# Two queues for the transposed blocks: SBUF-to-SBUF transfers issued by SP or ScalarE

## The chip, the cores and the metric

The kernel runs on one core of a Trainium2 chip. The metric is the device time of one execution in microseconds, median of several runs. The core has a matrix engine (TensorE, PE in the profile, its weight loads PEld), VectorE (DVE), ScalarE (ACT), GpSimd (POOL) and SyncE (SP). Each has its own instruction queue, which runs in order. DMAs are issued by instructions in the queues of SP and ScalarE and carried out by 16 DMA engines that all queues share; SP does nothing else in this kernel, while ScalarE also computes.

## The reference

Two layers (DEPTH = 2) of a decoder trunk, 512 positions of width 1024, in float32:

```python
mod = c_silu @ w_ada + b_ada                  # shift, scale, gate
u = rms_norm(x, norm_g) * (1 + scale) + shift
z = u @ w_in                                  # one projection, split for all mixers
ya = dsa_attention(rope(aq), rope(ak), av, rope(iq), rope(ik), iw) * silu(ag)
yb = swa_sinks_attention(rope(bq), rope(bk), bv, sinks) * silu(bg)
yc = stick_breaking_attention(cq, ck, cv) * silu(cg)
merged = sigmoid(ma) * (ya @ w_br_a) + sigmoid(mb) * (yb @ w_br_b) + sigmoid(mc) * (yc @ w_br_c)
x = x + gate * (merged @ w_out)
```

Mixer a has 8 heads of 64; an indexer scores the keys and each query attends, with a softmax, to its 128 best ones. Mixer b is a softmax attention over a window of 128 keys with a learned sink, 8 query heads on 2 key heads. Mixer c is a stick-breaking attention with 8 heads. A last RMSNorm follows.

## The kernel before

Activations lie transposed: features on the 128 partitions, the 512 positions along the free side. For precision every factor of a matrix product is split into a high and a low part of type float32r, and three products are added (high by high, high by low, low by high). So a weight block of 128x512 is loaded by a DMA (tile `wstage`, 4 buffers), cast to its high part (`whi`, on ScalarE, VectorE or GpSimd), and the rest is subtracted (`wlo`). PE then multiplies it with `uh` and `ul`, the two parts of u, into the banks `ps_z`.

The program has, for each layer, a first phase, a phase for the values, the mixers c, b and a, and the output projection. In the mixers several streams run woven together: the projections of the heads, the branches' products (`w_br_*`), the gates, the modulation of the next layer (`w_ss`, in layer 0), the indexer and its top-k (VectorE's max and match_replace on `score`), and the attention itself, pair of heads by pair of heads.

Queries and keys of the mixers a and b are rotated in `rope_evac` (L909-917): the projection is copied from its bank to `zs`, four DMAs swap the halves of each head from `zs` to `m2` (the profile calls it `m`), and VectorE or GpSimd combines them to `zc`, from which `Q` and `KH` are split.

For each of the four pairs of heads of mixers b and a, `softmax_qk` (L1262) computes the scores and the exponentials, and writes the normalised weights into one tile X (128 partitions, 1792 columns for b, 2560 for a; one buffer). Before they meet the values these weights must be transposed. `softmax_tr32` (L1356-1371) does it in two steps: VectorE transposes all 32x32 blocks within a quarter of X (4 instructions of 128x448 or 128x640), and after each of these 4 DMAs move 32 partitions of that quarter to another place in a tile U, or in `V5` (the profile calls it `V`) for the odd pairs. So a pair has 16 DMAs from SBUF to SBUF, 4 behind each transpose, all written as SP's. There are 2 layers x 2 mixers x 4 pairs = 16 such rows, 256 DMAs. The products with the values read U or V (`pairs`, L618). Mixer c transposes on PE (`softmax_tr`, L1372) and its rows have no such DMA. `TR32` (L47) says which pairs go through `softmax_tr32`: all four of a and all four of b.

The order is not that of the text. A `Recorder` takes each instruction with its alternatives (`add`, L317: a dictionary from engine to operation) and prices each one (`price`, L358). `forward` (L431) then plans the whole program: at each step the engine that can start an instruction earliest takes it, and among those ready the one with the earliest due time. An instruction with alternatives goes to the engine where it would end first (`elsewhere`, L558). For a DMA the price is the time on the issuing engine (`cost`) and the time of its bytes (`lag`, at 385 GB/s); its end is planned at L522-529, with a latency and behind the DMA before it. `LANES = 8`: the plan lets SP wait for the eighth DMA before it. `latest` computes due times from the plan, and `order` repeats this 5 times and keeps the plan that ends first. `emit` (L609) writes the instructions in that order, so each engine's queue is fixed. L620 is the line that emits nearly all of them, which is why most rows of the profile name it.

ScalarE issues 8 DMAs before, the stores `xsave<-xm` to HBM in `save`; all others are SP's.

Of the kernel before, what the change touches and what calls it, by code (L numbers as in the profile page):

```python
# [25 lines left out]
F32 = mybir.dt.float32  # L26
# [6 lines left out]
S = 512  # L33
P = 128
# [247 lines left out]
class Recorder:  # L282
# [75 lines left out]
    def price(self, x, engine, op, args, kw):  # L358

        y = Way()  # L360
        y.op, y.args, y.kw, y.mode, y.port = op, args, kw, None, False
        o = x.writes[0] if x.writes else None
        if op == "preload_act_table_set":
            y.cost = y.lag = 1.3
            return y
        if op == "dma_start":
            n = 1
            for d in (o or x.reads[0]).shape:
                n *= d
            y.cost, y.lag, y.mode = (0.58 if x.reads and x.writes and not x.reads[0].tile.pool.fixed else 0.36) if engine == "SP" else 0.1, n * 4 / 385e3, "dma"  # L370
            return y
        n = 1
        for d in o.shape[1:]:
            n *= d
        from_psum = any(v.tile.pool.name[:3] == "ps_" for v in x.reads)
        if engine == "PE":
            if op == "pairs":
                w = [int(np.prod(q[2].shape[1:])) for q in args]
                low, full = ([v for v, q in zip(w, args) if (q[2].dtype == F32) == t][::2] for t in (False, True))
                c, y.mode = sum(4 * v / 2.4e3 for v in full) + sum((v + 33) / 2.4e3 for v in low), "c" if full else "r"  # L380
                c += 0.37 if full and low else 0.26 if low else 0.21
                y.cost, y.lag = c, c + self.PIPE
            elif op == "transpose":
                c, y.mode = 0.1085, "t"
                y.cost, y.lag = c, c + self.PIPE
            else:
                rhs, y.mode = args[2], "m"
                c = 4 * n / 2.4e3 + 0.01 if rhs.dtype == F32 else 0.06 if rhs.dtype == BF16 else max(0.112, (n + 33.5) / 2.4e3)
                y.cost, y.lag = c, c + self.PIPE
            return y  # L390
        accum = "accum_out" in kw
        if engine == "ACT":
            b = 0.09 * sum(isinstance(kw.get(k), View) for k in ("bias", "scale"))
            c = 0.205 + 0.83e-3 * n + (b if not accum else 0.18) - (0.04 if from_psum else 0)
        elif engine == "DVE":
            y.port = not from_psum and op not in ("max", "match_replace", "memset", "reciprocal")
            if op == "tensor_tensor_scan":
                c = 1.21
            elif op == "max":
                c = 0.15 + 1.05e-3 * args[1].shape[-1]  # L400
            elif op == "match_replace":
                c = 0.215 + 1.045e-3 * args[2].shape[-1]
            elif n <= 16:
                c = 0.27 if op == "tensor_scalar" and len(x.reads) > 2 else 0.22 if op == "tensor_scalar" else 0.165 + (0.1 if accum else 0)
            elif op == "tensor_tensor_reduce":
                c = 0.147 + 1.05e-3 * n
            elif from_psum:
                c = 0.147 + 1.05e-3 * n + (0.08 if accum else 0)
            elif op in ("tensor_scalar", "tensor_copy"):
                c = 0.225 + 0.45e-3 * n if op == "tensor_scalar" else 0.16 + 0.52e-3 * n  # L410
            elif op == "memset":
                c = 0.1 + 0.6e-3 * n
            else:
                c = 0.15 + 1.05e-3 * n + (0.0 if accum else 0.06 if op == "scalar_tensor_tensor" else 0.0)
        else:
            y.port = n > 16
            if op == "memset":
                c = 0.12 if n < 16 else 0.52
            elif op == "tensor_copy":
                c = 0.2 + 0.82e-3 * n  # L420
            elif op == "tensor_scalar":
                c = 0.2 + 2.8e-3 * n
            else:
                c = 0.1 + 2.35e-3 * n
        y.cost, y.lag = c - self.OVERLAP[engine], c
        if engine != "POOL" and o.shape[0] < P:
            y.cost = c + (0.08 if engine == "DVE" else 0.02)
        return y


    def forward(self):  # L431
        E = {e: {"free": 0.0, "port": 0.0, "mode": None, "ready": {}, "pend": []} for e in self.real}
        dma_free, lanes = 0.0, []
# [36 lines left out]
        while len(out) < len(self.list):  # L470
            best = None
            for name, e in E.items():
# [5 lines left out]
                for i in list(ready):  # L478
                    x = ready[i]
# [3 lines left out]
                    y = x.alts[name]  # L483
                    at = max(free, port) if y.port else free
# [5 lines left out]
                if mine is None or mine[0] > free + 1e-9:  # L490
                    while pend and self.list[pend[0][1]].taken:
                        heapq.heappop(pend)
                    if pend:
                        est, i = pend[0]
                        x = self.list[i]
                        at = max(est, port) if x.alts[name].port else est
# [11 lines left out]
            e, x = E[name], self.list[i]  # L508
            y = x.alts[name]
# [12 lines left out]
            if y.mode == "dma":  # L522
                if not x.writes:
                    x.end = at + 2.1
                else:
                    x.end = dma_free = max(at + (2.1 if at < 20.0 else 3.0), dma_free) + y.lag * (1.2 if dma_free < 5.5 else 1.0)
                lanes.append(x.end)
                if name == "SP" and len(lanes) >= self.LANES:
                    e["free"] = max(e["free"], lanes[-self.LANES])
            else:  # L530
                x.end = at + y.lag + (hold - y.cost)
# [99 lines left out]
def op(cost, fn, *chunks):  # L631
    return ("op", cost, fn, [c + (phase[0],) for c in chunks])
# [15 lines left out]
def trunk(ctx, tc, xT, vecs, w_ss, w_gt, w_first, w_t, w_v, w_br, w_o, rope, consts, out):  # L648
# [7 lines left out]
    rec = Recorder(tc, nc, ps, sb)  # L656
    PE, ACT, DVE, POOL, SP = (rec.engine(e) for e in ("PE", "ACT", "DVE", "POOL", "SP"))
# [7 lines left out]
    def sbank():  # L665
        return rec.tile("ps_s", [P, S])
# [4 lines left out]
    def t512(tag, bufs=None, dt=F32):  # L671
        return rec.tile(tag, [P, S], dt)
# [38 lines left out]
    csb, o = small[:, 0:8], 8  # L711
    g_sb = [small[:, o + 8 * l:o + 8 * l + 8] for l in range(L)]
    fg_sb, o = small[:, o + 8 * L:o + 8 * L + 8], o + 8 * L + 8
    b_ada, o = [small[:, o + 24 * l:o + 24 * l + 24] for l in range(L)], o + 24 * L
    sink, o = small[:, o:o + 8 * L], o + 8 * L
# [59 lines left out]
    st = {}  # L775
# [560 lines left out]
    def blocks(b):  # L1336
        return 14 if b == "b" else 20
# [18 lines left out]
    def softmax_tr32(b, p):  # L1356
        def fn():
            pt = st.pop(("p", p))
            pos = bpos if b == "b" else apos
            N = blocks(b)  # L1360
            X = pt
            U = st["V5"][:, :N * P] if p % 2 and b in ('a', 'b') else rec.tile("U", [P, N * P], F32)
            n = N * 32
            for b_ in range(4):
                q = X[:, n * b_:n * b_ + n]
                DVE.transpose(q, q)
                for a_ in range(4):
                    SP.dma_start(U[32 * b_:32 * b_ + 32, n * a_:n * a_ + n], X[32 * a_:32 * a_ + 32, n * b_:n * b_ + n])
            st["pt", p] = U
        return op(1520 if b == "b" else 2180, fn)  # L1370

    def softmax_tr(b, p):  # L1372
        if p in TR32.get(b, ()):
            return softmax_tr32(b, p)

        def fn():
            pt = st.pop(("p", p))
            pos, tpos = (bpos, btpos) if b == "b" else (apos, cpos)
            nb = 4 if b == "b" else 5
            tb, PT, left = [None] * nb, [None] * nb, [0] * nb  # L1380
            for e in range(2):
                for j in range(4):
                    left[tpos(e, j)[0]] += 1
            for e in range(2):
                for j in range(4):
                    bk, c0 = tpos(e, j)
                    if tb[bk] is None:
                        tb[bk] = sbank()
                    for i in (range(j, min(4, j + 2)) if b == "b" else range(j, 4)):
                        sbk, s0 = pos(e, i)  # L1390
                        kc = s0 + 128 * j - keys(b, i)[0]
                        PE.transpose(tb[bk][:, c0 + 128 * (i - j):c0 + 128 * (i - j) + 128], pt[sbk][:, kc:kc + 128], ident)
                    left[bk] -= 1
                    if not left[bk]:
                        W = 384 if b == "b" and bk >= 2 else 512
                        if b == "c" and all(v is None for v in PT):
                            whole = rec.tile("U", [P, 5 * S], F32)
                        PT[bk] = whole[:, S * bk:S * bk + S] if b == "c" else t512("t", 10)
                        cast(PT[bk][:, :W], tb[bk][:, :W])
            st["pt", p] = PT  # L1400
        return op(1520 if b == "b" else 2180, fn)
# [402 lines left out]
```

## Time and profile before

| | |
|---|---|
| time, median of 3 runs | 1161.24 us (1161.12 to 1162.6) |
| the profiled execution | 1160.48 us, span 1158.7 us |
| mean granted clock of PE | 0.992 |
| PE busy | 1128.7 us (97%) |
| VectorE, ScalarE, GpSimd busy | 980.8, 547.0, 154.1 us |
| DMA moved | 157.23 MB, mean 136 GB/s |
| the chain that ended last | PE 79%, VectorE 12%, DMA 4%, SP's queue 2%, issue 2% |

The span is the time from the first to the last instruction. Busy PE means that a matmul is in its pipeline, not that it works at its peak. An instruction that issues a DMA is not counted as busy time of its engine; it shows in the timeline of the queue (SPq, ACTq), with the time that the issue took. The chain follows the work that ended last back to what released it at each step.

The mixers b and a lie at about 220 to 500 us in layer 0 and 800 to 1060 us in layer 1.

### The profile page before, as it was taken

Reading aid. Unit: us, or ns where it says so; the run is one execution under the profiler, and the core shown is the slowest. Engines: PE = TensorE matmul, PEld = TensorE weight load, DVE = VectorE, ACT = ScalarE, POOL = GpSimd, SP = SyncE. Lnnn points to the kernel's source line nnn. Section 1 sums busy time; section 2 is a strip of 40 time slices with the busy share of each in tenths; the row PEclk is TensorE's granted clock in tenths of the full one; section 3 lists DMA queues with packets and bytes.
Section 4 is the critical chain, followed back from the end, with each engine's and each line's share of the span. In section 5 each row is a group of like instructions: output and inputs, shape, how many; then the busy total and the mean of one; then the engine's idle time right before and its main releaser. Section 6 shows DMA issues by size and latency. Waiting matters only on the chain.

```text
span 1158.7 us, 17527 instructions
## 1 busy us (share of the span) xinstructions
PE 1128.7 (97%) x5619; PEld 935.8 (81%) x5619; DVE 980.8 (85%) x2223; ACT 547.0 (47%) x1150; POOL 154.1 (13%) x227
## 2 busy tenths in 40 slices
PE   8999999999997999999999999999999999999997
PEld 6899878888885777878898998888888777787886
DVE  7977999999998887878686689999999989776765
ACT  5623677653445552432143137765535456533222
POOL 0100345201012110000000004551000211000001
PEclk9999999999998999999999999999999999999999
DMA  9744323344454456555633342234445444535343
GB/s 346 234 117 128 97 77 92 109 144 129 129 161 144 140 158 174 148 166 165 188 120 108 103 134 82 82 92 124 130 146 142 132 108 137 160 107 145 95 126 107
DMA packets 92764, 157.23 MB, mean 136 GB/s; under 512 B 14080, under 2 KB 28672, under 8 KB 92672
## 3 DMA queue, kind: packets, MB, share of 16 engines
q1 hardware_dynamic: 91520, 154.02, 45.0%
q10 hardware_dynamic: 1152, 2.10, 0.5%
q8 instruction: 44, 0.72, 0.3%
q14 instruction: 48, 0.39, 0.1%
HBM read 125.39 MB, written 4.19 MB: 112 GB/s over the span
## 4 chain that ended last, share of the span: by engine, by line
PE 79%; DVE 12%; DMA 4%; SPq 2%; issue 2%; ACT 1%; POOL 0%; DVEq 0%; ACTq 0%
PE ps_z L620 60%; PE ps_s L620 15%; PE ps_s L618 3%; SPq L620 2%; DVE wlo L620 2%; DVE X L620 2%; PE ps_z L618 1%; DVE t L620 1%; DMA wstage<-in_w_t 1%; DVE zc L620 1%; DVE m L620 1%; DVE score L620 1%; DVE Q L620 1%; DMA Y<-in_w_ss 1%; DMA m<-zs 1%
## 5 line engine op out<-in xcount | busy, mean ns | idle before, releaser
L620 PE MATMUL ps_z<-uh,whi 128*128 128x512 f32 (+1 forms) x905 | 356.0, 395 | 10.4 <-DVE G L620 4.9
L620 PE MATMUL ps_z<-ul,whi 128*128 128x512 f32 (+1 forms) x905 | 354.2, 392 | 0.3 <-DVE ul L620 0.3
L620 PE MATMUL ps_z<-uh,wlo 128*128 128x512 f32 (+1 forms) x905 | 353.6, 392 | 0.0
L620 DVE TENSOR_TENSOR wlo<-wstage,whi 128x512 fp32r<-128x512 f32 (+2 forms) x329 | 215.1, 656 | 16.1 <-ACT whi L620 9.3
L620 PEld LDWEIGHTS ps_z<-uh,whi 128*128 128x128 f32 x905 | 170.9, 189 | 46.4 <-DVE G L620 5.2
L620 PEld LDWEIGHTS ps_z<-uh,wlo 128*128 128x128 f32 x905 | 171.0, 189 | 35.0 <-issue 0.7
L620 PEld LDWEIGHTS ps_z<-ul,whi 128*128 128x128 f32 x905 | 171.2, 189 | 34.5 <-issue 0.7
L620 ACT CAST whi<-wstage 128x512 fp32r<-128x512 f32 (+2 forms) x144 | 86.8, 606 | 154.7 <-PE ps_z L620 73.3
L620 DVE CAST whi<-wstage 128x512 fp32r<-128x512 f32 (+2 forms) x179 | 71.9, 402 | 94.2 <-PE ps_z L620 68.9
L620 PE MATMUL ps_z<-Y,whi 128*128 128x512 f32 x384 | 119.8, 392 | 1.3 <-DVE Y L620 1.0
L620 ACT ACTIVATE e<-ps_z 128x512 f32<-128x512 f32 x68 | 40.4, 595 | 105.7 <-PE ps_z L620 103.8
L620 PEld LDWEIGHTS ps_z<-Y,whi 128*128 128x128 f32 x384 | 72.3, 189 | 17.4 <-DVE Y L620 1.4
L620 ACT ACTIVATE e<-e 128x512 f32<-128x512 f32 x96 | 59.6, 629 | 45.5 <-DVE e L620 43.3
L620 ACT ACTIVATE t<-t,nm 128x256 f32<-128x256 f32 (+3 forms) x128 | 65.2, 511 | 21.6 <-DVE nm L620 21.6
L620 PE MATMUL ps_z<-Y,wlo 128*128 128x512 f32 x192 | 74.9, 390 | 0.0
L620 POOL CAST whi<-wstage 128x512 fp32r<-128x512 f32 (+1 forms) x49 | 29.9, 610 | 328.6 <-PE ps_z L620 229.8
L620 ACT ACTIVATE t<-t 128x512 f32<-128x512 f32 x120 | 67.2, 629 | 1.4 <-POOL zc L620 0.5
L620 POOL TENSOR_TENSOR wlo<-wstage,whi 128x512 fp32r<-128x512 f32 (+2 forms) x43 | 54.8, 1274 | 94.8 <-PE ps_z L620 61.8
L620 PE MATMUL ps_s<-KH,Q 128*128 128x256 f32 (+3 forms) x280 | 51.7, 305 | 5.9 <-DVE e L620 3.5
L620 DVE MAX8 m<-score 128x8 f32<-128x384 f32 (+2 forms) x96 | 53.2, 556 | 1.5
L620 PEld LDWEIGHTS ps_s<-KH,Q 128*128 128x128 f32 x280 | 42.7, 189 | 13.8 <-DVE e L620 4.3
L620 DVE MATCH_REPLACE8 score<-m,score 128x384 f32<-128x384 f32 (+2 forms) x96 | 52.0, 542 | 0.1
(220 smaller groups left out, 1947.1 us busy)
## 6 DMA issues: line engine op xcount, KB each, us to landing
wstage<-in_w_t SPq DMA_DIRECT2D x212, 256.0 KB, 2.7
wstage<-in_w_v SPq DMA_DIRECT2D x48, 182.0 KB, 2.3
m<-zs SPq DMA_DIRECT2D x128, 64.0 KB, 2.0
wstage<-in_w_gt SPq DMA_DIRECT2D x32, 256.0 KB, 2.7
wstage<-in_w_ss SPq DMA_DIRECT2D x32, 256.0 KB, 2.9
wstage<-in_w_o SPq DMA_DIRECT2D x32, 256.0 KB, 2.7
Y<-in_w_ss SPq DMA_DIRECT2D x15, 512.0 KB, 5.2
U<-X SPq DMA_DIRECT2D x64, 80.0 KB, 2.1
```

The source lines that it names most:

```text
L618: self.real[engine].matmul(*[real(a) for a in q[:3]], start=q[3], stop=True, skip_group_check=True)
L620: made = getattr(self.real[engine], y.op)(*[real(a) for a in y.args], **{k: real(v) for k, v in y.kw.items()})
```

## The change

The 16 DMAs of `softmax_tr32` are recorded with two alternatives, SP and ScalarE, with the same operation. The prices in `price` are made anew: on SP a DMA from SBUF to SBUF costs 0.63 (before 0.58) and any other 0.35 (0.36); on ScalarE it costs 0.63 or 0.35 (before 0.1 for all); on GpSimd 1.0 (no DMA is recorded for it). The planned end of a DMA that takes under 0.22 us for its bytes is 2.2 us after the issue plus these bytes, before 3.0; that holds for the rope copies (64 KB, 0.17 us) and for the moves of X (56 KB, 0.15 us, and 80 KB, 0.21 us). In `softmax_tr` two conditions are written more generally; for the mixers a and b the function has already returned `softmax_tr32` there, and for c both forms say the same.

```diff
@@ price, L367
-            y.cost, y.lag, y.mode = (0.58 if x.reads and x.writes and not x.reads[0].tile.pool.fixed else 0.36) if engine == "SP" else 0.1, n * 4 / 385e3, "dma"
+            y.cost, y.lag, y.mode = (0.63 if x.reads and x.writes and not x.reads[0].tile.pool.fixed and not o.tile.pool.fixed else 0.35) if engine == "SP" else 1.0 if engine == "POOL" else 0.63 if x.reads and not o.tile.pool.fixed else 0.35, n * 4 / 385e3, "dma"
@@ forward, L523
-                    x.end = dma_free = max(at + (2.1 if at < 20.0 else 3.0), dma_free) + y.lag * (1.2 if dma_free < 5.5 else 1.0)
+                    x.end = dma_free = max(at + (2.1 if at < 20.0 else 2.2 if y.lag < 0.22 else 3.0), dma_free) + y.lag * (1.2 if dma_free < 5.5 else 1.0)
@@ softmax_tr32, L1365
                 for a_ in range(4):
-                    SP.dma_start(U[32 * b_:32 * b_ + 32, n * a_:n * a_ + n], X[32 * a_:32 * a_ + 32, n * b_:n * b_ + n])
+                    how = ("dma_start", (U[32 * b_:32 * b_ + 32, n * a_:n * a_ + n], X[32 * a_:32 * a_ + 32, n * b_:n * b_ + n]), {})
+                    rec.add({"SP": how, "ACT": how})
@@ softmax_tr, L1393
-                        if b == "c" and all(v is None for v in PT):
-                            whole = rec.tile("U", [P, 5 * S], F32)
-                        PT[bk] = whole[:, S * bk:S * bk + S] if b == "c" else t512("t", 10)
+                        if all(v is None for v in PT):
+                            whole = st["V5"] if b != "c" and p % 2 else rec.tile("U", [P, 5 * S], F32)
+                        PT[bk] = whole[:, S * bk:S * bk + S]
```

## The prediction

> **What bounds the kernel now.** I read the page first, then the busy times by stage, then what TensorE (PE) waits for, and last the queue of SP where PE had stopped.
>
> ```profile
> span 1158.7 us, 17527 instructions
> ...
> PE 1128.7 (97%) x5619; PEld 935.8 (81%) x5619; DVE 980.8 (85%) x2223; ACT 547.0 (47%) x1150; POOL 154.1 (13%) x227
> ```
>
> PE is busy for 97% of the span, so a change that leaves the matmuls alone can only win what PE stands idle, or runs at a lower clock. By stage (columns: span, busy time of PE, PEld, DVE, ACT, POOL, granted clock, DMA share, GB/s):
>
> ```profile
> 340.00:440.00 100.00, 89.64 (x416) 68.75 (x415) 82.83 (x202) 49.67 (x114) 16.16 (x18) 0.93 0.52 149
> ...
> 800.00:900.00 100.00, 99.58 (x478) 82.10 (x478) 96.01 (x260) 50.29 (x125) 5.80 (x8) 1.00 0.47 138
> 900.00:960.00 60.00, 54.98 (x271) 42.88 (x270) 50.52 (x108) 28.45 (x63) 12.52 (x14) 1.00 0.46 126
> ```
>
> Inside the mixers b and a PE loses 10.4 us between 340 and 440 (layer 0) and 5.0 us between 900 and 960 (layer 1). Its waits, first from 220 to 500, then from 800 to 1060 (total, times, longest):
>
> ```profile
> PE ps_z L620 <- DVE G L620: 4.9, 1, 4.9
> PE ps_z L620 <- ACT whi L620: 2.8, 2, 2.5
> PE ps_s L620 <- DVE e L620: 2.4, 1, 2.4
> ```
>
> ```profile
> PE ps_z L620 <- ACT whi L620: 1.8, 1, 1.8
> PE ps_s L620 <- ACT KH L620: 1.2, 1, 1.2
> PE ps_s L620 <- DVE e L620: 1.1, 1, 1.1
> ```
>
> Four of these six stand right behind one thing in SP's queue: 16 transfers of the transposed X, issued in one row (start, duration, count).
>
> ```profile
> 332.74 10.03 SPq L620 DMA_DIRECT2D V<-X  x16
> 342.87 2.43 SPq L620 DMA_DIRECT2D m<-zs  x4
> ...
> 346.02 3.54 SPq L620 DMA_DIRECT2D m<-zs  x4
> ...
> 404.71 10.38 SPq L620 DMA_DIRECT2D V<-X  x16
> ...
> 418.34 0.40 SPq L620 DMA_DIRECT2D wstage<-in_w_t  x1
> ...
> 906.36 11.09 SPq L620 DMA_DIRECT2D V<-X  x16
> 917.55 2.44 SPq L620 DMA_DIRECT2D m<-zs  x4
> ...
> 942.25 10.83 SPq L620 DMA_DIRECT2D U<-X  x16
> ...
> 955.71 1.02 SPq L620 DMA_DIRECT2D wstage<-in_w_t  x2
> ```
>
> A row of 16 holds SP for 10.0 to 11.1 us, 0.63 us each (10.03 / 16), and the rope copies (m<-zs) and weight loads wait behind it. How that reaches PE, at 348.7 us, on ScalarE and VectorE (start, duration, in brackets the idle time before):
>
> ```profile
> 336.27 0.58 ACT L620 COPY zs<-ps_z 128x512 f32<-128x512 f32 x1
> 340.95 0.59 ACT L620 COPY zs<-ps_z 128x512 f32<-128x512 f32 x1 [4.10 <-PE ps_z L620]
> ```
>
> ```profile
> 332.04 1.16 DVE L620 STREAM_TRANSPOSE X<-X 128x448 f32<-128x448 f32 x2
> ...
> 334.97 0.65 DVE L620 STREAM_TRANSPOSE X<-X 128x448 f32<-128x448 f32 x1
> ...
> 336.98 0.64 DVE L620 STREAM_TRANSPOSE X<-X 128x448 f32<-128x448 f32 x1
> ...
> 348.69 0.69 DVE L620 TENSOR_TENSOR m<-m,rt 128x512 f32<-128x512 f32 x1 [1.79 <-DMA m<-zs]
> ```
>
> The first zs is there at 336.9 and its copy is issued at 342.87; the second is there at 341.5 and its copy goes at 346.02. VectorE then idles 1.79 us for it, and PE 2.4 us.
>
> **The change part by part.** *The choice of queue.* There are 256 such issues (two groups of 128 below), in 16 rows of 16; each may now go to SP or ScalarE, to whichever the plan expects to end it first.
>
> ```profile
> L620 SPq DMA_DIRECT2D U<-X x128: 507/588/1815, 232.5 to 1004.8; - x128
> L620 SPq DMA_DIRECT2D V<-X x128: 507/588/1730, 255.8 to 1055.7; - x128
> ```
>
> The issue on ScalarE isn't in the trace for this kind. The nearest rows bound it: 0.33 us for ScalarE's own store to HBM (below), 0.59 us for this transfer on SP, 1.8 us for the longest of those. I take 0.63 us with the gap, SP's price, since it is the same transfer. ScalarE has room: over the 16 rows' spans (two of them, then all together) it is busy 71.77 of 168.80 us.
>
> ```profile
> 404.70:415.10 10.40, 10.40 (x48) 8.61 (x47) 10.37 (x31) 7.54 (x22) 3.07 (x3) 1.00 0.60 162
> ...
> 942.20:953.10 10.90, 10.90 (x49) 9.02 (x49) 8.65 (x14) 4.73 (x8) 0.00 (x0) 1.00 0.48 122
> ...
> sum 168.80, PE 166.53 PEld 137.54 DVE 149.20 ACT 71.77 POOL 15.30; mean PE 10.41 PEld 8.60 DVE 9.32 ACT 4.49 POOL 0.96
> ```
>
> Free are 97 us, 6.1 a row, or 9 issues at 0.63. All four issues behind a transpose come ready together with SP mostly free, so SP takes the first and the two alternate: I expect 6 to 8 of 16 on ScalarE, 7 x 16 = 112 in all, and a row that takes 5.5 to 7 us on SP, 3 to 5 us less.
>
> What that frees: (a) the copy behind the row at 332.74 can go once the last transpose (336.98 + 0.64 = 337.6) has had its two issues on SP, at 338.9 instead of 342.87, and the second copy when its zs is there, 4.5 us earlier: more than the wait of 2.4, which goes. (b) At 917.55 the same, 1.1 us. (c) The weight load at 955.71, behind the row at 942.25 where ScalarE is busy only 4.73 of 10.9 us: 1.8 us. (d) The load at 418.34, behind the row at 404.71: there ScalarE is busy 7.54 of 10.4, so 4 issues move at most, 2.5 us, against waits of 2.5 + 0.3; I count half, 1.4. After (a) and (d) the clock was also halved:
>
> ```profile
> 352.60:356.00 3.40, 3.40 (x13) 2.80 (x13) 3.35 (x6) 2.78 (x6) 0.00 (x0) 0.51 0.47 154
> 424.40:427.70 3.30, 3.30 (x9) 2.54 (x8) 2.84 (x6) 1.69 (x3) 0.00 (x0) 0.50 0.54 132
> ```
>
> 3.4 us at half speed lose 1.7 us each; I count 1.7 for (a) and half, 0.85, for (d). The Trainium skill, "TensorE: Matmul & The Clock Gate" (Part 1: The HAM clock gate), lets the clock fall after an idle window of about 3.4 us; the rows show it fall after waits of 2.4 and 2.5 us. By the page's figure the two would be worth nothing in the clock and the sum 2.6 us later; the measured rows decide here. Together (a) to (d) free 2.4 + 1.7 + 1.1 + 1.8 + 1.4 + 0.85 = 9.2 us. (e) The 4.9 us wait for DVE G and (f) the 1.2 us for KH hang on VectorE's and ScalarE's own queues; I count 0, with (e) and its clock worth up to 8 us if the 1.79 us that VectorE lost before it ripple through.
>
> What it costs: 112 x 0.63 = 70 us of ScalarE, hidden in its 97 idle us as a sum, but its queue runs in order. An issue waits for its transpose, and behind it stand casts of weights (whi), the exponentials of the softmax and the casts of Q and KH, for which PE waited above 1.2 to 2.5 us at a time. Below, the cost is nothing if the plan puts each issue where the transpose is done; above, it is 16 rows x 2.4 us = 38 us, 2.4 being the time between the second and third transposes of the row at 332.7 (ended 333.2 and 335.6; 332.04 + 1.16 and 334.97 + 0.65). I take one row in four with a wait of 1.1 us, like the shorter ones above: 4.4 us, rounded to 4. It is nearer to the lower end because ScalarE idles more than it works there.
>
> *The prices.* SP's cost of an SBUF-to-SBUF issue goes from 0.58 to 0.63, of a load from 0.36 to 0.35, ScalarE's from 0.1 to 0.35 or 0.63, and a small transfer lands at 2.2 us plus its bytes instead of 3.0:
>
> ```profile
> U<-X SPq DMA_DIRECT2D x64, 80.0 KB, 2.1
> ```
>
> ```profile
> L620 ACTq DMA_DIRECT2D xsave<-xm x8: 326/332/354, 551.5 to 590.8; - x8
> ```
>
> These are nearer to the rows than before. They add no instruction, but every order is made anew from them. What a new order is worth the two layers show, with the same work and two orders: 10.4 and 5.0 us of idle PE. So I take 0, with 5.4 us to either side. *The last hunk* changes no instruction: for a and b the function has returned before it, and for c the tile is the one it was.
>
> The Trainium skill, "DMA: Bandwidth & Descriptors" (Issuing engines are not separate DMA queues), speaks against the change: several issuers share the same DMA engines and save only issue time, usually small beside the transfer. Here 0.59 us of issue stand against 2.1 us of landing, but sixteen in a row take 10 us. If that rule's "small" held, the 9.2 us would be 0.
>
> Sum: 1160.48 us is the profiled execution (span 1158.7 and 1.8 around it); 1160.48 - 9.2 + 4 = 1155.3. It lies 0.76 below the median of 1161.24, so the forecast is 1156.
>
> **The rivals.** *ScalarE is held (slower).* Issues that wait for late transposes keep whi casts and exponentials back, and PE then waits 2.4 us and runs at half clock after it, 1.7 more: 4.1 a row. From the third such row on the 9.2 us are eaten; with four, 16.4 - 9.2 = 7 us, 1168. For it: PE already waited for ACT four times (whi twice, whi, KH, above), and ScalarE is busy 7.54 of 10.4 us in one row. Against it: its mean there is 43%. *VectorE takes over.* It is busy 96.01 of 100 us from 800 to 900; with SP's waits gone the same matmuls wait for VectorE, and what is freed and what is lost cancel: 1160. Against it: at 348.69 VectorE itself waited for SP's copy. *Transfers, not issues, set the landing.* Two queues then interleave on the same DMA engines and everything lands as late as now: 1161. Against it: DMA share of 0.48 and 0.60 in the two rows shown. *The plan hardly uses ScalarE*, since SP is free when a transpose ends and ScalarE's other work is more urgent; only the prices act: 1161, 5.4 to either side. *All goes well*: (a) to (e) whole, 2.4 + 1.7 + 1.1 + 1.8 + 2.8 + 1.7 + half of 8, and no loss on ScalarE: 15 us, 1146.
>
> **How the numbers follow.** Forecast 0.45, ScalarE held 0.24, VectorE takes over 0.14, transfers 0.03, hardly used 0.07, all goes well 0.07. Within 0.2%, about what a measurement of this kernel can tell, is 1158.9 to 1163.6. Faster: 0.42 of the forecast, 0.07 of the best case, 0.03 of the others, 0.52. Slower: 0.24 and 0.06 of the new orders, 0.30. Same: 0.18. The likeliest one's own range is 1151 to 1161 (5.4 for the order); for 8 in 10 it reaches from the best case to the held ScalarE and a little over: 1146 to 1170.
>
> **What will show it.** Right: 90 to 130 issues of U and V<-X on ScalarE's queue, the row of 16 at 5.5 to 7 us on SP, about 0.6 us per issue on ScalarE, no half clock after the waits (a) and (d), PE's idle time between 340 and 440 under 6 us. Wrong: fewer than 50 on ScalarE; issues there above 1 us; new PE waits for ACT whi, KH or t of over 2 us; or idle PE in the mixers at 15 us again with SP free, which would mean VectorE.

## The result and the profile after

The changed kernel takes 1144.05 us (1142.08 to 1145.32) against 1161.74 us (1161.12 to 1162.6): ratio 0.9846, 95% interval 0.9828 to 0.9863. It is faster, as forecast, but by 17.7 us (1.5%) where 5.2 were forecast, and the time is 2 us below the range. The profiled execution (1142.08 us) has a span 18.4 us shorter. Two lines of its page:

```profile
span 1140.3 us, 17580 instructions
...
PE 1123.2 (99%) x5619; PEld 932.7 (82%) x5619; DVE 984.5 (86%) x2238; ACT 530.2 (46%) x1125; POOL 169.4 (15%) x237
```

The same 5619 matmuls; PE's idle time falls from 30.0 us (1158.7 - 1128.7) to 17.1 us, which is 12.9 of the 18.4. The other 5.5 us are busy time, and nearly all of that is the clock. The stages with the mixers b and a show both (columns as before):

```profile
340.00:440.00 100.00, 96.08 (x461) 74.20 (x460) 92.73 (x228) 47.84 (x110) 17.33 (x18) 0.98 0.56 164
900.00:960.00 60.00, 59.49 (x300) 47.29 (x299) 58.49 (x141) 31.34 (x72) 16.84 (x18) 1.00 0.50 143
```

PE idles 3.9 us (before 10.4) and 0.5 us (before 5.0), and the granted clock in the first stage is 0.98 instead of 0.93, worth (0.98 - 0.93) x 100 = 5 us. The moves of X, by queue (issue time in ns, min/median/max):

```profile
L620 ACTq DMA_DIRECT2D U<-X x74: 514/554/1562, 237.4 to 983.9; - x74
L620 ACTq DMA_DIRECT2D V<-X x70: 514/556/855, 257.2 to 1032.1; - x70
...
L620 SPq DMA_DIRECT2D V<-X x58: 507/575/840, 257.2 to 1032.5; - x58
L620 SPq DMA_DIRECT2D U<-X x54: 507/570/1352, 237.4 to 985.0; - x54
```

The plan gave 144 of the 256 to ScalarE, 9 of 16. The spans of the 16 rows sum to 118.2 us, 7.4 each, before 168.8 and 10.6 (busy time of each engine in them):

```profile
sum 118.20, PE 115.65 PEld 96.28 DVE 112.43 ACT 17.86 POOL 15.12; mean PE 7.23 PEld 6.02 DVE 7.03 ACT 1.12 POOL 0.94
```

ScalarE is busy 17.86 of these 118.2 us, before 71.77 of 168.8: in the new order most of its other work lies outside the rows. The row of layer 0 that I followed in the prediction, on SP's queue and on ScalarE's:

```profile
331.17 5.87 SPq L620 DMA_DIRECT2D V<-X  x9
337.14 2.45 SPq L620 DMA_DIRECT2D m<-zs  x4
...
345.43 2.41 SPq L620 DMA_DIRECT2D m<-zs  x4
```

```profile
331.14 0.52 ACTq L620 DMA_DIRECT2D V<-X  x1
331.71 0.62 ACT L620 CAST KH<-zc 64x512 fp32r<-64x512 f32 x1 [2.74 <-DVE zc L620]
332.27 1.23 ACTq L620 DMA_DIRECT2D V<-X  x2
...
334.30 2.45 ACTq L620 DMA_DIRECT2D V<-X  x4
```

The row takes 5.9 us and the rope copies follow at 337.14, 0.6 us after their zs; before it was 6.0. Summed over the 28 groups of rope copies behind projections, the time from the end of the copy to zs to the first issue fell from 60.6 to 20.0 us. PE's waits, the two longest from 220 to 500, and the only one from 800 to 1060:

```profile
PE ps_z L620 <- DVE sm L620: 2.2, 1, 2.2
PE ps_z L620 <- DVE zc L620: 1.6, 1, 1.6
```

```profile
PE ps_s L620 <- DVE e L620: 0.5, 1, 0.5
```

None of the waits behind SP's rows is left, and the wait of 4.9 us for DVE G, which I had left standing, is gone too. What is left is VectorE's. The clock falls once, to 0.50 from 418.5 to 421.9 us, after the 2.2 us for `sm`; that wait ends at 418.06, and on VectorE three transposes of X stand in front of `sm`:

```profile
415.14 2.29 DVE L620 STREAM_TRANSPOSE X<-X 128x640 f32<-128x640 f32 x3
417.36 0.65 DVE L620 TENSOR_TENSOR sm<-ps_z,sm 128x512 f32<-128x512 f32 x1
```

### The profile page after: what moved, and what is told of

Its sections match the earlier page's. It is cut to its first block, busy times and chain, and to the rows that moved or that the text cites. A ratio compares the mean times of both kernels' runs of the same rounds, so it can differ in the third digit from the quotient of the medians.

```text
span 1140.3 us, 17580 instructions
## 1 busy us (share of the span) xinstructions
PE 1123.2 (99%) x5619; PEld 932.7 (82%) x5619; DVE 984.5 (86%) x2238; ACT 530.2 (46%) x1125; POOL 169.4 (15%) x237
## 4 chain that ended last, share of the span: by engine, by line
PE 82%; DVE 11%; DMA 2%; issue 2%; ACT 1%; SPq 0%; POOL 0%; DVEq 0%; ACTq 0%; POOLq 0%
PE ps_z L620 64%; PE ps_s L620 15%; DVE t L620 3%; PE ps_s L618 3%; DVE m L620 1%; DVE score L620 1%; DVE wlo L620 1%; PE ps_z L618 1%; DVE X L620 1%; DMA Y<-in_w_ss 1%; DVE zc L620 1%; DVE Y L620 1%; DVE e L620 0%; SPq L620 0%; DMA V<-X 0%
## 5 line engine op out<-in xcount | busy, mean ns | idle before, releaser
L620 DVE TENSOR_TENSOR wlo<-wstage,whi 128x512 fp32r<-128x512 f32 (+2 forms) x322 | 210.8, 657 | 12.4 <-ACT whi L620 4.5
L620 DVE CAST whi<-wstage 128x512 fp32r<-128x512 f32 (+1 forms) x200 | 81.0, 406 | 89.3 <-PE ps_z L620 72.7
L620 ACT CAST whi<-wstage 128x512 fp32r<-128x512 f32 (+2 forms) x122 | 73.0, 601 | 112.6 <-PE ps_z L620 67.7
L620 POOL TENSOR_TENSOR wlo<-wstage,whi 128x512 fp32r<-128x512 f32 (+2 forms) x50 | 63.8, 1277 | 138.6 <-PE ps_z L620 52.3
L620 DVE MAX8 m<-score 128x8 f32<-128x256 f32 (+2 forms) x96 | 53.2, 554 | 1.4
L620 DVE MATCH_REPLACE8 score<-m,score 128x256 f32<-128x256 f32 (+2 forms) x96 | 52.0, 542 | 0.1
```

The source lines that it names most:

```text
L620: made = getattr(self.real[engine], y.op)(*[real(a) for a in y.args], **{k: real(v) for k, v in y.kw.items()})
```

## The experiments

Theory Q: the gain is SP's queue made free. Theory O: it is the new order that the new prices make. Theory H, from the prediction's rivals: ScalarE is held by what it issues. Four kernels take the change apart.

**Prices alone.** The choice is taken out again:

```diff
-                    rec.add({"SP": how, "ACT": how})
+                    rec.add({"SP": how})
```

> The new prices with all 256 moves of X left to SP. Theory Q (the gain is SP's queue made free: 16 issues in a row no longer hold up rope copies and weight loads): SP still takes 10 us a row, so 1161 us within 6, and PE waits behind the rows. Theory O (the gain is the new order that the new prices, above all the earlier landing, give): 1144 to 1150 us.

Measured: 1159.7 us, ratio 0.9982 (0.9965 to 0.9999). PE waits as before, in part longer (the two longest of 220 to 500 us):

```profile
PE ps_z L620 <- DVE G L620: 5.0, 1, 5.0
PE ps_z L620 <- DVE whi L620: 3.8, 1, 3.8
```

O falls in this form: the prices without the choice are worth 0.2%.

**The choice alone**, with the old prices and the old landing:

```diff
-            y.cost, ... = (0.63 if ... else 0.35) if engine == "SP" else ...
+            y.cost, ... = (0.58 if ... else 0.36) if engine == "SP" or <move of X> else 0.1, ...
-        max(at + (2.1 if at < 20.0 else 2.2 if y.lag < 0.22 else 3.0), dma_free)
+        max(at + (2.1 if at < 20.0 else 3.0), dma_free)
```

> The choice between SP and ScalarE with the old prices: 0.58 for a move of X on either queue, landing 3.0. Theory Q: 1144 to 1150 us, 100 to 150 moves on ScalarE, rows of 16 in 6 to 9 us. Theory O: 1156 to 1162 us, as the prices that made the order are the old ones.

Measured: 1146.53 us, 0.9855 (0.9828 to 0.9883), 138 moves on ScalarE. Nothing measurable separates it from the changed kernel. The choice has the gain, through the queue or through the order that is planned with it; the next two kernels part these.

**The changed kernel's order on one queue.** Only the queue of the emitted issue is changed:

```diff
+                at = self.real["SP"] if y.op == "dma_start" and len(x.alts) > 1 else self.real[engine]
-                made = getattr(self.real[engine], y.op)(...)
+                made = getattr(at, y.op)(...)
```

> The changed kernel's order of all instructions, kept as it is, but its 144 moves of X on ScalarE are issued by SP, at the same place in the order. Theory Q: the rows take 10 us again and the rope copies wait, at least as slow as before, 1160 to 1175 us, since this order was made for two queues. Theory O: 1144 to 1150 us.

Measured: 1195.01 us, 1.0291 (1.025 to 1.0332), slower by more than Q expected. In this kernel PE waits (first two of 220 to 500, then the third of 800 to 1060):

```profile
PE ps_s L621 <- DVE KH L621: 5.8, 1, 5.8
PE ps_z L618 <- DMA U<-X: 4.3, 1, 4.3
```

```profile
PE ps_z L618 <- DMA m<-zs: 3.3, 1, 3.3
```

The order by itself is worth nothing on one queue. It puts rope copies between the moves (SP takes 14.7 us for its first row), and PE waits for the moved blocks themselves: 4.3 us for U above, and 6.8 us in all for V.

**The old order on two queues.** Nothing is planned anew; at emission every second move of X goes to ScalarE:

```diff
+                if y.op == "dma_start" and engine == "SP" and x.reads and x.reads[0].tile.pool.name == "X":
+                    self.moved = getattr(self, "moved", 0) + 1
+                    at = self.real["ACT"] if self.moved % 2 == 0 else at
```

> The old kernel's order, kept as it is, but every second move of X is issued by ScalarE at the same place in the order. Theory Q: the four waits behind SP's rows (2.4, 2.8, 1.1, 1.8 us) and their half clock go at least in part, 1148 to 1156 us. Theory O: 1160 to 1163 us. Rival H (ScalarE is held by issues that wait for their transposes): above 1163 us, as nothing in this order makes room for them.

Measured: 1146.5 us, 0.9863 (0.984 to 0.9886), better than Q expected; the total shows nothing of H at this share. So the queue has 15 of the 17.7 us with every instruction in its old place. How far it goes I measured with the same edit and other shares: a quarter (`% 4 == 0`), three quarters (`% 4 != 1`), all.

> The old kernel's order kept, and one of the four moves behind each transpose issued by ScalarE (4 of 16). Theory Q: a row takes 12 x 0.63 = 7.6 us on SP, about half the way to the split by two, so half of its gain or more: 1149 to 1155 us. Theory H (ScalarE is held): the cost grows with the issues moved, so this one is the best of the series.

> The old kernel's order kept, three of four moves on ScalarE (12 of 16, 7.6 us of ScalarE a row in a place not made for it). Theory Q alone: SP is held only 2.5 us a row, 1143 to 1147 us. Theory H: 1150 to 1160 us.

> The old kernel's order kept, all 256 moves on ScalarE. Theory Q alone: SP is never held, 1143 to 1147 us. Theory H: each row holds ScalarE 10 us as it held SP, and the casts of weights and keys behind it come as late as the copies did: 1158 to 1180 us.

| moves of 16 on ScalarE, old order | us | ratio |
|---|---|---|
| 0 (before) | 1161.7 | 1 |
| 4 | 1145.61 | 0.9864 (0.9846 to 0.9882) |
| 8 | 1146.5 | 0.9863 (0.984 to 0.9886) |
| 12 | 1156.17 | 0.9952 (0.9934 to 0.9971) |
| 16 | 1174.96 | 1.0131 (1.0096 to 1.0166) |

The quarter came out better than Q gave for it, and 12 and 16 where H put them. So a quarter is enough: the whole gain lies in the first 4 issues. Between 4 and 8 the medians differ by less than the runs of one kernel do; against 8, 10 us are lost at 12 and 28 us at 16. That loss is as large as H gave; what makes it was not separated. The quarter's row on SP, where the rope copies now go at 337.92:

```profile
329.85 7.96 SPq L624 DMA_DIRECT2D V<-X  x12
337.92 2.43 SPq L624 DMA_DIRECT2D m<-zs  x4
```

With a quarter PE waits from 220 to 500 us only this (the wait for DVE G stays in the old order); with all of them on ScalarE, the rows take 10.1 to 13.3 us as they did on SP, and PE waits from 800 to 1060 us:

```profile
PE ps_z L624 <- DVE G L624: 4.9, 1, 4.9
PE ps_z L624 <- ACT whi L624: 1.3, 2, 1.0
```

```profile
PE ps_s L624 <- ACT KH L624: 2.2, 1, 2.2
PE ps_s L624 <- DVE KH L624: 2.0, 1, 2.0
PE ps_s L624 <- DVE Q L624: 1.7, 1, 1.7
PE ps_z L618 <- DMA U<-X: 1.7, 1, 1.7
```

**More in the plan.** Four kernels plan further steps: the rope copies behind projections free to go to either queue as well; ScalarE's price for a move 0.95 instead of 0.63; the plan's wait for the eighth DMA before held against ScalarE too; a fixed quarter (`"ACT" if a_ == 3 else "SP"`) instead of the choice; and beside the last three the changed kernel once more.

```diff
-            SP.dma_start(m2[a:a + 32], zs[b:b + 32])
+            how = ("dma_start", (m2[a:a + 32], zs[b:b + 32]), {})
+            rec.add({"SP": how, "ACT": how})
```

> The changed kernel with the 112 rope copies behind the projections also free to go to either queue, at the same prices. In the changed kernel these copies still wait 20 us in all behind other issues, and PE waits 4.6 us in the mixers b and a. Theory Q: 1138 to 1144 us. Theory H: up to 56 issues more on ScalarE, 1146 to 1155 us.

```diff
-    ... else 0.63 if x.reads and not o.tile.pool.fixed else 0.35, n * 4 / 385e3, "dma"
+    ... else 0.95 if x.reads and not o.tile.pool.fixed else 0.35, n * 4 / 385e3, "dma"
```

> The changed kernel with ScalarE's price of a move of X at 0.95 in place of 0.63, so that fewer than 144 go there, some 80 to 120. If what a move costs ScalarE matters beyond its issue time (4 and 8 of 16 gave the same time in the old order, 12 and 16 lost 10 and 28 us), 1139 to 1144 us; if the flat part between 4 and 8 holds here too, 1143 to 1147 us.

```diff
-                if name == "SP" and len(lanes) >= self.LANES:
+                if len(lanes) >= self.LANES:
```

> The changed kernel with the plan's wait for the eighth DMA before it held against ScalarE's queue too. If ScalarE is held at its issues by earlier DMAs (issues of 1 us and over on its queue in the changed kernel), the plan now sees it: 1138 to 1143 us. If not, 1142 to 1147 us.

```diff
-                    rec.add({"SP": how, "ACT": how})
+                    rec.add({"ACT" if a_ == 3 else "SP": how})
```

> The changed kernel with a fixed share in place of the choice: the fourth move behind each transpose is ScalarE's (64 in all), the others SP's, and the order is planned with that. If the plan's choice by the free queue is worth something over a fixed quarter: 1146 to 1155 us. If not, as the old order with a quarter moved: 1142 to 1147 us.

> The changed kernel once more, on the chip of these runs, to compare them with: 1142 to 1146 us by every theory.

| planned with | us | ratio |
|---|---|---|
| rope copies on either queue | 1158.47 | 0.9978 (0.9963 to 0.9993) |
| ScalarE at 0.95 (90 moves there) | 1154.33 | 0.9931 (0.9904 to 0.9958) |
| wait for the eighth DMA on both | 1148.58 | 0.9892 (0.9871 to 0.9913) |
| a fixed quarter | 1157.93 | 0.9972 (0.9957 to 0.9986) |
| the changed kernel again | 1144.67 | 0.9857 (0.9839 to 0.9875) |

All four variants are slower than the changed kernel, by 4 to 14 us, and all came out above what any theory had given for them. The fixed quarter is the plainest: planned for its share it takes 1157.93 us, while the old order with the same share takes 1145.61. So I crossed orders with shares:

> The order of the prices-only kernel (planned with all moves on SP, 1159.7 us with them there), kept, with every second move issued by ScalarE. If the gain is that of the split in any order planned for SP alone: 1143 to 1147 us. If the old order was a lucky one for it: 1148 to 1156 us.

> The order of the planned quarter (1157.9 us), kept, with every second move on ScalarE. If its slowness is its order: 1153 to 1160 us again. If it is its share of SP (12 of 16): 1143 to 1149 us.

> The changed kernel's order, kept, with every second move on ScalarE instead of the 144 that the plan chose. If the choice by the free queue is what the change is worth: 1150 to 1165 us, between the 1144 of the chosen and the 1195 of SP alone. If any split by two does: 1143 to 1148 us.

> The order of the prices-only kernel, kept, with every fourth move on ScalarE. As with the old order (1145.6 us with a quarter): 1143 to 1148 us. If the old order was a lucky one: 1150 to 1157 us.

Every one of these kernels keeps the named order and sets the queue at emission, as above.

| order | as planned | a quarter on ScalarE | a half |
|---|---|---|---|
| old | 1161.7 | 1145.61 | 1146.5 |
| prices alone | 1159.7 | 1149.41 (0.9892) | 1149.74 (0.9899) |
| planned for a quarter | (a quarter) | 1157.93 | 1148.01 (0.9879) |
| changed kernel | 1144.67 (9 of 16, chosen) | | 1149.65 (0.9901) |

With a half, every order ends between 1146.5 and 1149.7. The old order was a lucky one for the split, by 3 to 4 us beside that of the prices alone: 1149.74 lies where this case had been put, while 1149.41 and 1149.65 fall between the two cases given for each. The plan's own choice gains 5 us over an even half in its own order (1149.65 to 1144.67), but not over the old order. The slow order of the planned quarter is cured by giving SP less: its rope copies wait 51.4 us in all with 12 of 16 on SP and 21.7 with the half, where those of the old order with 12 of 16 wait 33.2. PE's waits from 220 to 500 us are 9.7 us in all as planned and 5.5 with the half; the longest, in this order:

```profile
PE ps_z L620 <- ACT whi L620: 2.8, 1, 2.8
PE ps_s L620 <- DVE e L620: 2.2, 1, 2.2
```

```profile
PE ps_z L624 <- ACT whi L624: 2.2, 1, 2.2
PE ps_z L624 <- DVE zc L624: 1.7, 1, 1.7
PE ps_z L624 <- DVE wlo L624: 1.3, 1, 1.3
```

Why the kernels with free rope copies and with the higher price lose 14 and 10 us against the changed one stays open: share and order changed together there.

## Why the prediction was right and wrong

Right were the mechanism and the direction: SP's rows of 16 held rope copies and weight loads, and sharing them frees PE. The row's length fell from 10.6 to 7.4 us (5.5 to 7 expected, 5.9 in the row followed). More moves went to ScalarE than the 112 I had counted: 144. An issue there took 0.555 us without the gap behind it (on SP 0.57); four in a row took 2.45 us, 0.61 each, where 0.63 was expected.

The old order with a share moved lets the sum be checked term by term, because its matmuls come in the same sequence as before: I took the start of the same matmul in both traces and noted, by stretches of the old kernel's time, how much the difference grows (us gained, clock included).

| step of the sum (stretch, us) | forecast | a quarter | a half |
|---|---|---|---|
| (a) copies behind the row at 332.7 (340 to 364) | 4.1 | 4.1 | 2.3 |
| (b) 922 (914 to 930) | 1.1 | 1.9 | 1.9 |
| (c) 957 (945 to 962) | 1.8 | 1.3 | 1.3 |
| (d) 419.8 (414 to 440) | 2.25 | 2.6 | 0.6 |
| (e) DVE G (364 to 400) | 0 | -0.1 | 0.7 |
| (f) KH, 908 (900 to 914) | 0 | 1.5 | 1.5 |
| waits not in the sum (250, 502, 823, 937, 992, 1058) | 0 | 4.2 | 4.1 |
| the first 30 us and the rest | 0 | 0.2 | 0.6 |
| ScalarE's cost | -4 | in the rows above | in the rows above |
| sum | 5.2 | 15.7 | 13.0 |

The profiled spans differ by 15.8 and 13.0 us, so the rows are the whole gain. (a) to (d) give 9.9 us with the quarter, where the sum had 9.2.

**The step that failed** is the term that I put at nothing: (f) and the small waits. I had counted only waits of over 1 us of the two mixer stages and had put (f) down to ScalarE's own queue. They are worth 5.6 us at both shares, 1.5 for (f) and 4.1 for the others, more than the whole forecast gain. Those that I followed stand behind the other rows in the same way: the one at 250 behind the row that began at 232.5, that at 823 behind the one at 805.0, and that at 502 behind the row at 484.00. The load of `w_ss`, the fourth behind that row, lands at 500.6 us; VectorE waits for it and comes to PE's operand Y only then:

```profile
484.00 10.01 SPq L620 DMA_DIRECT2D V<-X  x16
...
495.68 0.38 SPq L620 DMA_DIRECT2D wstage<-in_w_ss  x1
```

Most of them lie outside the two stages that I had looked at, where before the idle time looked small (with the row of 800 to 900 us in the prediction, 0.8 + 1.0 + 0.4 us):

```profile
220.00:340.00 120.00, 119.19 (x565) 98.40 (x564) 116.18 (x317) 63.80 (x158) 10.54 (x12) 1.00 0.46 138
...
440.00:560.00 120.00, 118.99 (x534) 96.81 (x533) 94.40 (x218) 41.23 (x77) 0.61 (x1) 1.00 0.55 162
```

The starts of the matmuls show up to 0.4 us more at most of these places than the idle time does, since a matmul counts as busy while it is in the pipeline: a wait of 1.0 us at 502 gave 1.3 us when it went.

A second term was mis-sized for the changed kernel, the 4 us for ScalarE. With a quarter in the old order no such cost is seen. With a half, whose 128 moves are nearest to my 112, (a) and (d) give back 3.8 us, about what I had put down, so at that share the price itself was near. But in the changed kernel, with 144 moves, no wait of PE from 220 to 500 or 800 to 1060 us names ScalarE, which does little else during the rows there (17.86 of 118.2 us). That is the lower end of what I had given for this term.

The order I took as 0 with 5.4 us to either side. In the changed kernel the wait (e) for DVE G went whole, 4.9 us and 3.4 us of clock, which I had put at 0; it stays in the old order with shares and is missing when the changed kernel's order runs on one queue, so the new order took it away and not the freed copies. The same order brought new waits from 220 to 1060 us: 2.2 us for `sm` with 1.7 us of clock, 1.6 for `zc`, and three of 0.4 to 0.5 us, 6.9 us in all. So the order gained 8.3 - 6.9 = 1.4 us, and the changed kernel ends 1 to 2 us below the old order with shares. That the order came out near 0 is luck in part: my 5.4 us came from two stages that I called the same work, but they are 100 and 60 us long and only layer 0 has `w_ss`, and kernels planned anew then differed by up to 14 us.

The rivals. *ScalarE is held*: a loss of the size that it gave shows from 12 of 16 on, not from a few unlucky rows; the plan stayed at 9. *VectorE takes over*: in part. Between 340 and 440 us it went from 82.83 to 92.73 us busy, and most of the 6.9 us of new waits are its own, but they did not cancel the gain. *Transfers set the landing*: the landing did grow, from 2.1 to between 2.3 and 2.9 us for the 80 KB moves, but no wait of PE in the two mixer stretches names a transfer:

```profile
V<-X ACTq DMA_DIRECT2D x38, 80.0 KB, 2.3
U<-X ACTq DMA_DIRECT2D x34, 80.0 KB, 2.9
U<-X SPq DMA_DIRECT2D x30, 80.0 KB, 2.8
...
V<-X SPq DMA_DIRECT2D x26, 80.0 KB, 2.4
```

The rule of the Trainium skill, "DMA: Bandwidth & Descriptors" (Issuing engines are not separate DMA queues), says that the queues share the engines and that only issue time is saved; the longer landing fits the first, and the split in the old order the second. Its remark that this time is usually small beside the transfer holds for one move (0.59 us beside 2.1 us), but not for the row: 16 issues took 10 us, and what stood behind the rows was worth some 15 us. The nearest case was "all goes well" (1146, a chance of 0.07), and that it came so near is luck: it counted half of (e)'s 8 us, which went whole, none of the small waits, and no new waits.

## What to carry to other kernels

Where a queue issues many small transfers in a row, look at what stands behind the row, sum all waits of the engine that sets the end in those stages and not only the long ones, and move a quarter to a half of the row to another queue: the first few issues bring most, the last ones cost more than they bring. Try it first at emission with the order kept; it tells the queue's worth from that of a new order, which here could take 12 us of it away (a quarter on ScalarE: 1145.61 us in the old order, 1157.93 us planned anew). A change to a planner's prices and alternatives re-makes everything, so one planned variant says little on the idea.

## What the runs showed of the hardware

**An issue on ScalarE's queue costs its engine little when an activation runs.** In the kernel with all moves on ScalarE, its queue without issues and with them (start, duration):

```profile
401.38 0.60 ACT L624 ACTIVATE t<-t,nm 128x384 f32<-128x384 f32 x1
401.88 0.19 ACT L624 ACTIVATION_READ_ACCUMULATOR t<-t,nm 128x1 f32 x1
401.98 0.49 ACT L624 ACTIVATE t<-t,nm 128x256 f32<-128x256 f32 x1
...
402.47 0.39 ACT L624 ACTIVATE t<-t,nm 128x128 f32<-128x128 f32 x1
...
413.81 0.60 ACT L624 ACTIVATE t<-t,nm 128x384 f32<-128x384 f32 x1
413.81 0.55 ACTq L624 DMA_DIRECT2D V<-X  x1
414.31 0.19 ACT L624 ACTIVATION_READ_ACCUMULATOR t<-t,nm 128x1 f32 x1
414.41 0.51 ACT L624 ACTIVATE t<-t,nm 128x256 f32<-128x256 f32 x1
414.46 0.55 ACTq L624 DMA_DIRECT2D V<-X  x1
414.82 0.19 ACT L624 ACTIVATION_READ_ACCUMULATOR t<-t,nm 128x1 f32 x1
415.06 0.40 ACT L624 ACTIVATE t<-t,nm 128x128 f32<-128x128 f32 x1
```

From the activation of 384 columns to that of 256 it is 0.60 us without an issue between (401.38 to 401.98) and 0.60 with one (413.81 to 414.41): the issue of 0.55 us runs beside the activation. From 256 to 128 columns it is 0.49 us without an issue (401.98 to 402.47) and 0.65 with one (414.41 to 415.06); here the activation of 0.51 us is shorter than the issue. Over the whole traces, the places where one issue lies between two such activations lose this much against the same pair without one: at most 0.02 us in all 8 places with a quarter of the moves on ScalarE; at most 0.02 us in 9 of 10 and 0.75 us in one with a half; up to 0.16 us in 12 of 15 and 0.24, 0.29 and 0.72 us in the others with all. So an issue cost mostly 0 to 0.16 us there, not 0.63. In the changed kernel no issue lies between two such activations, so this price is not shown for it. What made the larger shares slow is then hardly the time of the issues themselves: the row again takes 10 us and more on one queue, and PE waits for U and for Q and KH. That was not separated further.

**The clock.** Before, it fell to one half after waits of PE of 2.4, 2.5 and 4.9 us, and not after those of 1.1 and 1.8 us. No sharp bound lies between: with a half of the moves in the old order it fell after one of 1.9 us, in the changed kernel after one of 2.2 us, and with the choice at the old prices it did not fall in the mixers after one of 2.0 us. Before, each of these falls lasted 3.4 us, or twice that around the wait of 4.9 us.
